# The recurrent layers of a streaming encoder on one core: 12 channel tiles of 112 against 10 of 126 and one of 84, with the gates' bias as a row

## The chip, the cores and the metric

The kernel runs on one core of a Trainium2 chip. Its engines are named PE (TensorE, matrix products), ACT (ScalarE), DVE (VectorE), POOL (GpSimd) and SP (SyncE, which here issues most of the DMA). The metric is the device time of one execution in microseconds (us); the time of a kernel is the median of several runs.

## The reference

Four layers over 256 frames of 1024 channels, batch 1. Each layer is a token mixer, a cross-attention into 256 memory tokens and a squared-ReLU MLP, each followed by `x <- LayerNorm(alpha*x + f(x))`. Layers 0 and 3 use the recurrent mixer, layer 1 a delta-rule mixer, layer 2 chunked attention. The recurrent mixer is the part that matters here; it has 1344 channels in 16 blocks of 84:

```python
u = x @ w_in                                     # 1024 -> 2 * 1344
gate_branch = gelu(u[..., :1344])
xr = causal_depthwise_conv(u[..., 1344:], conv_w, conv_b)        # 4 taps
xb = xr.reshape(bsz, seq, 16, 84)
gates = einsum('bsnc,gncd->bsgnd', xb, gate_w) + gate_b          # two gates, block-diagonal
r_gate, i_gate = sigmoid(gates)
log_a = -8 * r_gate * softplus(-lam)
a = exp(log_a)
b = sqrt(-expm1(2 * log_a)) * (i_gate * xr)
h_t = a_t * h_{t-1} + b_t                                        # scan over the frames
y = (h * gate_branch) @ w_out                    # 1344 -> 1024
```

## The kernel before

All weights come from HBM in chunks of up to 128 x 1024 float32. For each chunk ACT writes a rounded half `whi` (line 455) and DVE the rest `wlo` (line 456); a product is then three matmuls in the type fp32r, whi with both halves of the activation and wlo with the first (lines 273 to 275, `mm_piece`). `Stream` keeps up to seven split chunks: `done(i)` of a chunk lets the next be split and the raw buffer of a later one be loaded on SP's queue. Everything is issued in an order written out by hand, and each engine works through its own list in that order.

A recurrent layer (`lru`) runs over the channels in 12 tiles of 112 (`CT`), in 4 groups of 3. Three x pieces and three gelu pieces of 448 columns (`x_piece`, `g_piece`), each four chunks and two halves of 128 frames, make the two branches. `conv(i)` transposes four tiles of an x piece (line 796), ACT starts the convolution with its bias (line 802) and DVE adds three taps. `gates(g)` computes both gates of three tiles. As a block of 84 channels crosses the edges of tiles of 112, a group has seven products of 112 x 112 x 256 per gate (`GPAIRS`, line 842), in float32, into a bank of the pool `mm` (two banks); ACT adds the bias in the sigmoid and computes a tanh, per tile. The pool `acc` has four banks, `tp` two. The weights of groups 0 and 1 are loaded on SP's queue after the first x piece, those of groups 2 and 3 on ACT's queue in the middle of `gates(0)` and `gates(1)`.

`decay` and `scan` (exp, square, sqrt, DVE's scan) are issued between the halves of the gelu pieces. Last, `mem_piece` (products of the memory tokens, line 314) is drained in portions between the groups of transposes of the gelu branch (line 926); DVE multiplies (line 929), the result is split, and `out_gemm` makes the output product, 12 row tiles of 112.

In the first layer the memory tokens are loaded after the third x piece and split (`mem_split`, memhi and memlo) after `gelu(1)`; in the second recurrent layer after the first and second x piece. `lru_c`, once at the start, computes cc = -8 softplus(-lam) with a long list of small operations on POOL. `chunks` counts calls: at the sixth, the third gelu piece of the first layer, it issues the load of x itself for the residual and of the norm's two vectors.

Of the kernel before, what the change touches and what calls it, by code (L numbers as in the profile page):

```python
# [16 lines left out]
T = 256  # L17
# [3 lines left out]
CT = 112  # L21
NT = DR // CT
GPAIRS = [(0, 0), (1, 0), (0, 1), (1, 1), (2, 1), (1, 2), (2, 2)]
# [11 lines left out]
LV = 0  # L35
# [31 lines left out]
class Stream:  # L67
# [46 lines left out]
    def _split(self):  # L114
# [13 lines left out]
        for c in self._cols(i, f):  # L128
            k.split(raw[:p, c], hi[:p, c], lo[:p, c])
# [34 lines left out]
    def done(self, i):  # L164
# [68 lines left out]
class Kern:  # L233
# [20 lines left out]
    def mm_piece(self, acc, chunks, lhs, p, w, kpc=2, kt0=0, start=True, stop=True, last=False, near=None):  # L254
# [4 lines left out]
        for ci, c in enumerate(chunks):  # L259
            if not self.dry:  # L260
                wh, wl = self.st.hl[c]
                for k in range(kpc):
# [5 lines left out]
                    kt = kt0 + ci * kpc + k  # L268
                    a, b = lhs(kt)
                    ws = slice(k * w, (k + 1) * w)  # L270
# [393 lines left out]
    def out_gemm(self, name, idx, n, lhs, p):  # L664

        for nh in range(2):
            a = [self.acc(), self.acc()]
            parts = [range(n)] if n <= 4 else [range(n // 2), range(n // 2, n)]
            for part in parts:
                end = part is parts[-1]  # L670
                ch = [self.st.take(name, (*idx, nh, q), p, 1024) for q in part]
                last = end and nh == 1
                near = self.next_ht() if last else None
                for t in range(2):
                    self.mm_piece(a[t], ch, lhs[t], p, 512, kt0=2 * part[0], start=part[0] == 0, stop=end,
                                  last=t == 1 and not last, near=near if t else None)
# [98 lines left out]
    def lru(self, l, j):  # L775
        nc, tc = self.nc, self.tc
        with tc.tile_pool(name="lru", bufs=1, reuse_waits="tile") as p:
# [3 lines left out]
            nat = {}  # L781

            def x_piece(i):
                for t, a in self.gemm("lru_in", (j, 3 + i), 4, self.hT, 128, 448):
                    s = gn[t][:, 896:] if i == 2 else p.tile([128, 448], F32, name="xn", tag="CB"[i], bufs=4)
                    nc.scalar.copy(s, a[:, :448])
# [4 lines left out]
            def conv(i):  # L791
                for b in range(2):
                    ps = self.tp()
                    for q in range(2):
                        for t in range(2):
                            nc.tensor.transpose(ps[:CT, q * T + t * 128:q * T + t * 128 + 128],
                                                nat[i, t][:, (2 * b + q) * CT:(2 * b + q + 1) * CT], self.ident)
# [1145 lines left out]
```

## Time and profile before

| | us |
|---|---|
| median of 3 runs | 1813.78 (1811.99 to 1815.51) |
| the profiled execution | 1802.43 |
| its span, first to last instruction | 1800.6 |
| PE busy in it | 1736.4 (96%) |
| DVE, ACT, POOL busy | 1252.3, 871.6, 55.3 |

The stages of the first recurrent layer lie, in us from the start of the span, at 5.4 to 41.8 (x branch), to 69.2 (gates), to 100.1 (gelu branch), to 118.9 (product with the gelu branch and memory products) and to 151.6 (output product); the second recurrent layer's gates lie at 1406.5 to 1435.6 and its gelu branch at 1435.6 to 1466.1.

The mean granted clock of TensorE in that execution is 0.995 of its full 2.4 GHz. The time of one profiled execution stands below the median; it is its own run.

### The profile page before, as it was taken

How to read it: one execution, taken by the hardware profiler on the slowest of the kernel's cores; microseconds unless marked ns; L12 is line 12 of the kernel's file. 1: busy time of each engine (PE TensorE's matmuls, PEld its weight loads, DVE VectorE, ACT ScalarE, POOL GpSimd, SP SyncE). 2: the span in 40 equal slices, each digit the busy share in tenths (PEclk: the TensorE clock that was granted, in tenths of full speed). 3: DMA queues.
4: the chain of work that ended last, by engine and by line, in shares of the span. 5: the costliest groups of instructions: out<-in, count | busy, mean ns of one | idle time of the engine just before them, and what ended most of it. 6: DMA issues, size and time to landing. Idle time of an engine off the chain costs nothing.

```text
span 1800.6 us, 25667 instructions
## 1 busy us (share of the span) xinstructions
PE 1736.4 (96%) x10032; PEld 1453.8 (81%) x10032; DVE 1252.3 (70%) x1809; ACT 871.6 (48%) x1338; POOL 55.3 (3%) x64
## 2 busy tenths in 40 slices
PE   8999999999999989999999999999999999999998
PEld 7888988888777656888887888888888887988886
DVE  6587776667578798776667567776667587677665
ACT  6754534444543134544444544634444674545442
POOL 2000000000000001000000000000000000000000
PEclk9999999999999999999999999999999999999999
DMA  7464555555242224455555623545555545636552
GB/s 243 138 205 175 186 185 192 187 187 202 95 144 86 91 93 137 151 187 194 189 190 197 244 94 119 186 164 187 187 188 189 168 147 164 208 120 231 186 187 94
DMA packets 92927, 302.39 MB, mean 168 GB/s; under 512 B 11906, under 2 KB 19586, under 8 KB 92676
## 3 DMA queue, kind: packets, MB, share of 16 engines
q1 hardware_dynamic: 91780, 297.92, 49.3%
q10 hardware_dynamic: 1024, 2.81, 0.5%
q8 instruction: 79, 1.29, 0.3%
q14 instruction: 44, 0.36, 0.1%
HBM read 299.65 MB, written 1.05 MB: 167 GB/s over the span
## 4 chain that ended last, share of the span: by engine, by line
PE 78%; DVE 11%; ACT 4%; DMA 4%; issue 2%; POOL 0%; SPq 0%; DVEq 0%; ACTq 0%
PE acc L275 12%; PE acc L273 12%; PE acc L274 12%; PE tp L294 5%; PE mm L294 5%; PE acc L314 4%; PE acc L294 4%; PE acc L517 4%; PE tp L295 3%; PE mm L295 3%; DVE wlo L456 2%; PE acc L192 2%; PE mm L842 2%; PE tp L352 2%; PE acc L295 2%
## 5 line engine op out<-in xcount | busy, mean ns | idle before, releaser
L456 DVE TENSOR_TENSOR wlo<-wraw,whi 128x1024 fp32r<-128x1024 f32 (+3 forms) x505 | 593.7, 1206 | 133.3 <-ACT whi L455 121.9
L455 ACT CAST whi<-wraw 128x1024 fp32r<-128x1024 f32 (+3 forms) x505 | 507.2, 1039 | 163.5 <-PE acc L275 97.3
L273 PE MATMUL acc<-whi,ahi 128*128 128x512 f32 x512 | 200.3, 391 | 0.0
L275 PE MATMUL acc<-whi,alo 128*128 128x512 f32 x512 | 199.7, 390 | 0.0
L274 PE MATMUL acc<-wlo,ahi 128*128 128x512 f32 x512 | 199.4, 389 | 0.0
L273 PE MATMUL acc<-whi,ht 128*128 128x448 f32 (+1 forms) x368 | 142.4, 387 | 5.5 <-ACT whi L455 5.5
L274 PE MATMUL acc<-wlo,ht 128*128 128x448 f32 (+1 forms) x368 | 140.6, 382 | 3.5 <-DVE wlo L456 3.5
L275 PE MATMUL acc<-whi,ht 128*128 128x448 f32 (+1 forms) x368 | 140.4, 381 | 0.0
L294 PE MATMUL tp<-ht,whi 128*128 128x512 f32 x384 | 136.7, 398 | 0.0
L294 PE MATMUL mm<-ht,whi 128*128 128x512 f32 x384 | 136.5, 398 | 0.0
L294 PE MATMUL acc<-ht,whi 128*128 128x512 f32 x352 | 126.0, 400 | 1.9 <-DVE qkT L987 1.9
L275 PEld LDWEIGHTS acc<-whi,alo 128*128 128x128 f32 x512 | 96.1, 188 | 20.9
L273 PEld LDWEIGHTS acc<-whi,ahi 128*128 128x128 f32 x512 | 96.1, 188 | 20.2
L274 PEld LDWEIGHTS acc<-wlo,ahi 128*128 128x128 f32 x512 | 96.2, 188 | 19.2
L295 PE MATMUL tp<-ht,wlo 128*128 128x256 f32 x384 | 107.9, 281 | 0.0
L295 PE MATMUL mm<-ht,wlo 128*128 128x256 f32 x384 | 107.8, 281 | 0.0
L295 PE MATMUL acc<-ht,wlo 128*128 128x256 f32 x352 | 98.7, 280 | 0.0
L734 DVE TENSOR_TENSOR rel<-mm,rel 128x256 f32<-128x256 f32 x48 | 18.6, 425 | 110.4 <-ACT rel L733 110.4
L355 ACT CAST ht<-tp 128x512 fp32r<-128x512 f32 x40 | 22.8, 589 | 135.3 <-PE tp L352 134.3
L738 ACT CAST ahi<-rel 128x512 fp32r<-128x512 f32 x56 | 34.8, 622 | 110.0 <-DVE rel L737 110.0
L294 PEld LDWEIGHTS tp<-ht,whi 128*128 128x128 f32 x384 | 72.2, 188 | 18.0
L294 PEld LDWEIGHTS mm<-ht,whi 128*128 128x128 f32 x384 | 72.1, 188 | 17.6
(387 smaller groups left out, 3419.3 us busy)
## 6 DMA issues: line engine op xcount, KB each, us to landing
wraw<-in_w SPq DMA_DIRECT2D x256, 512.0 KB, 4.5
wraw<-in_w_kv SPq DMA_DIRECT2D x64, 512.0 KB, 4.3
wraw<-in_lru_in SPq DMA_DIRECT2D x47, 448.0 KB, 4.7
wraw<-in_w_q SPq DMA_DIRECT2D x32, 512.0 KB, 4.3
wraw<-in_w_co SPq DMA_DIRECT2D x32, 512.0 KB, 4.7
wraw<-in_ca_qkv SPq DMA_DIRECT2D x24, 512.0 KB, 4.5
wraw<-in_lru_out SPq DMA_DIRECT2D x24, 448.0 KB, 5.0
ln_gt<-in_ln_g SPq DMA_DIRECT2D x12, 512.0 KB, 6.1
```

Source lines behind the costliest of these rows:

```text
L192: return f(*a, **k)
L273: nc.tensor.matmul(acc[:, :w], lhsT=a, rhs=wh[:p, ws], start=s, stop=False)
L274: nc.tensor.matmul(acc[:, :w], lhsT=a, rhs=wl[:p, ws], start=False, stop=False)
L275: nc.tensor.matmul(acc[:, :w], lhsT=b, rhs=wh[:p, ws], start=False, stop=e)
L294: self.nc.tensor.matmul(four, lhsT=wh[:, ws], rhs=xy, start=s, stop=False)
L295: self.nc.tensor.matmul(four[:, :2], lhsT=wl[:, ws], rhs=x, start=False, stop=e)
L314: self.nc.tensor.matmul(a, lhsT=w[:, ws], rhs=v, start=s and i == 0, stop=e and i == 2)
L352: self.nc.tensor.transpose(dst_ps[:n, j * p:(j + 1) * p], s, self.ident[:p, :p])
L455: self.nc.scalar.copy(hi, src)
L456: self.nc.vector.tensor_tensor(out=lo, in0=src, in1=hi.bitcast(F32), op=ALU.subtract)
L517: nc.tensor.matmul(a, lhsT=u, rhs=w[:, ws], start=s, stop=e)
L842: nc.tensor.matmul(ps[:CT, gate * T:(gate + 1) * T], lhsT=gw[gate][:, n, :], rhs=xc[g][:, k, :], start=n == ks[0][0], stop=n == ks[-1][0])
```

## The change

The channels of the recurrent layers are reordered when the weights are laid out. Three blocks of 84 make two tiles of 126: each tile has one whole block and one half (42 channels) of the third, the first tile's half at rows 0 to 41, the second tile's at rows 64 to 105. Five such pairs and the last block alone, 84, make 11 tiles, in groups of 4, 4 and 3. A tile's gates are then one full product, and for each pair and gate two products of 42 rows bring what the divided block owes to the other tile. The tiles of xc have one row more, which holds 1.0; the gate weights hold the bias in that row. All pieces are 504 or 336 columns, and `mm_piece` steps over a pitch of 64 so that the split halves of 504 columns lie at a pitch of 512. The output product ends in a chunk of one short tile. Order: gates(0), conv(2), tanh(0), (first layer: mem_split), gates(1), tanh(1), gates(2), tanh(2). Sigmoid runs on both gates of a tile at once, cc is multiplied in by DVE, tanh and exp run on a whole group.

```diff
-CT = 112
-NT = DR // CT
-GPAIRS = [(0, 0), (1, 0), (0, 1), (1, 1), (2, 1), (1, 2), (2, 2)]
+CT = 126
+NT = 11
+LB = 84
+LW = 504, 504, 336
...
+        w = f // 2
+        if _pitch(w) == w or f <= 512:
+            for c in self._cols(i, f):
+                k.split(raw[:p, c], hi[:p, c], lo[:p, c])
+        else:
+            for q in ((0, 1), (1, 2)) if i == 0 else ((0, 2),):
+                at = lambda x, n: x[:p, :2 * n].rearrange("p (k w) -> p k w", w=n)[:, q[0]:q[1], :w]
+                k.split(at(raw, w), at(hi, _pitch(w)), at(lo, _pitch(w)))
...
+def _pitch(w):
+    return -(-w // 64) * 64
...
+                if tail and ci == n - 1:
+                    p, kpc, ci0 = tail, 1, 2 * ci
+                else:
+                    ci0 = ci * kpc
...
-                    ws = slice(k * w, (k + 1) * w)
+                    ws = slice(k * _pitch(w), k * _pitch(w) + w)
...
+            tiles = 4, 4, 3
+            wide = lambda c: LB if c == NT - 1 else CT
...
-            xc = [p.tile([CT, 3, T], F32, name="xc", tag="A", bufs=4) for _ in range(4)]
+            xc = [p.tile([CT + 1, n, T], F32, name="xc", tag=f"A{g}") for g, n in enumerate(tiles)]
+            for x in xc:
+                nc.gpsimd.memset(x, 1.0)
...
             def load_gw(g, queue):
-                gws.append([])
-                for gate in range(2):
-                    w = p.tile([CT, 7, CT], F32, name="gw", tag="gw", bufs=4)
-                    queue.dma_start(w, self.I["lru_gw"][j, g, gate])
-                    gws[g].append(w)
+                m = tiles[g] + tiles[g] // 2
+                w = p.tile([CT + 1, 2, m * CT], F32, name="gw", tag=f"gw{g}")
+                queue.dma_start(w, self.I["lru_gw"][j, g, :, :, :m * CT])
+                gws.append(w)
 
             def gates(g):
-                for o in range(3):
-                    ps = self.acc() if LV & 8 else self.mm()
-                    ks = [(n, k) for n, (k, oo) in enumerate(GPAIRS) if oo == o]
+                n, gw = tiles[g], gws[g]
+                r = p.tile([CT, 2, n, T], F32, name="ri", tag=f"B{g}")
+                for b in range(2):
+                    os = range(2 * b, min(2 * b + 2, n))
+                    bank = (self.mm, self.acc)[b]
+                    pss = [bank() for _ in os]
                     for gate in range(2):
-                        for n, k in ks:
-                            nc.tensor.matmul(ps[:CT, gate * T:(gate + 1) * T], lhsT=gw[gate][:, n, :], rhs=xc[g][:, k, :],
-                                             start=n == ks[0][0], stop=n == ks[-1][0])
-                    c = 3 * g + o
-                    nc.scalar.activation(r[:, o, :], ps[:CT, :T], AF.Sigmoid, bias=par[:, c, 6:7])
-                    nc.scalar.activation(it[:, o, :], ps[:CT, T:], AF.Sigmoid, bias=par[:, c, 7:8])
-                    nc.scalar.activation(h[:, o, :], r[:, o, :], AF.Tanh, scale=cc[:, c:c + 1])
-                nc.vector.tensor_tensor(out=xc[g], in0=xc[g], in1=it, op=ALU.mult)
-                if g < 2:
-                    load_gw(g + 2, nc.scalar)
+                        gs = slice(gate * T, (gate + 1) * T)
+                        for o, ps in zip(os, pss):
+                            nc.tensor.matmul(ps[:CT, gs], lhsT=gw[:, gate, o * CT:(o + 1) * CT], rhs=xc[g][:, o, :],
+                                             start=True, stop=len(os) == 1)
+                        if len(os) == 1:
+                            continue
+                        w = slice((n + b) * CT, (n + b + 1) * CT)
+                        for u in range(2):
+                            a = slice(64 * u, 64 * u + 42)
+                            nc.tensor.matmul(pss[1 - u][:CT, gs], lhsT=gw[a, gate, w], rhs=xc[g][a, 2 * b + u, :], start=False, stop=True)
+                    for o, ps in zip(os, pss):
+                        nc.scalar.activation(r[:, :, o, :], ps[:CT, :].rearrange("p (g t) -> p g t", g=2), AF.Sigmoid)
+                v = r[:, 0, :n, :]
+                nc.vector.tensor_tensor(out=v, in0=v, in1=cc[:, 4 * g:4 * g + n].unsqueeze(2).to_broadcast([CT, n, T]), op=ALU.mult)
+                x = xc[g][:CT, :n, :]
+                nc.vector.tensor_tensor(out=x, in0=x, in1=r[:, 1, :n, :], op=ALU.mult)
+                ri.append(r)
+
+            def tanh(g):
+                nc.scalar.activation(ri[g][:, 1], ri[g][:, 0], AF.Tanh)
...
             x_piece(0)
-            for g in range(2):
+            for g in range(3):
                 load_gw(g, nc.sync)
...
-            else:
-                conv(2)
-                gates(1)
...
+            gates(0)
+            conv(2)
+            tanh(0)
+            if l == 0:
+                self.mem_split()
+            gates(1)
+            tanh(1)
             gates(2)
-            gates(3)
...
-            else:
-                g0 = g_piece(0, lambda t: (decay(2 * t), decay(2 * t + 1)))
+            tanh(2)
+            g0 = g_piece(0, lambda t: (decay(0), decay(1)) if t == 0 else decay(2))
...
-            else:
-                g1 = g_piece(1, lambda t: (scan(2 * t), scan(2 * t + 1)))
+            g1 = g_piece(1, lambda t: (scan(0), scan(1)) if t == 0 else scan(2))
             gelu(0, gn)
             gelu(1, g1)
-            if l == 0:
-                self.mem_split()
             gelu(2, g_piece(2))
...
-            self.out_gemm("lru_out", (j,), 6, [lhs(0), lhs(1)], CT)
+            self.out_gemm("lru_out", (j,), 6, [lhs(0), lhs(1)], CT, tail=("lru_out2", LB))
```

## Rows read from the trace of the kernel before

**Rows 1.** Page, part 1: busy us of each engine, share, instructions.

```profile
PE 1736.4 (96%) x10032; PEld 1453.8 (81%) x10032; DVE 1252.3 (70%) x1809; ACT 871.6 (48%) x1338; POOL 55.3 (3%) x64
```

**Rows 2.** Windows: PE, PEld, DVE, ACT, POOL busy, granted clock, DMA share, GB/s.

```profile
5.40:41.80 36.40, 34.91 (x160) 30.04 (x161) 26.25 (x43) 22.84 (x36) 10.64 (x24) 1.00 0.82 269
41.80:69.20 27.40, 25.38 (x121) 20.35 (x120) 12.34 (x21) 17.86 (x40) 0.00 (x0) 1.00 0.53 157
69.20:100.10 30.90, 29.80 (x146) 27.10 (x145) 23.68 (x29) 29.08 (x42) 0.00 (x0) 1.00 0.39 135
100.10:118.90 18.80, 16.00 (x121) 15.60 (x120) 15.01 (x19) 7.73 (x11) 0.00 (x0) 0.91 0.74 222
118.90:151.60 32.70, 32.23 (x144) 26.39 (x142) 23.93 (x29) 13.81 (x16) 1.00 (x1) 1.00 0.64 200
1406.50:1435.60 29.10, 27.14 (x123) 22.02 (x122) 14.60 (x27) 20.41 (x43) 0.00 (x0) 0.94 0.42 138
1435.60:1466.10 30.50, 29.41 (x145) 26.80 (x144) 23.62 (x29) 27.40 (x40) 0.00 (x0) 1.00 0.39 129
```

**Rows 3.** Timeline of PE in the first layer's gates: start, us, instruction, count.

```profile
47.92 1.04 PE L796 MATMUL tp<-ident,gn 128*112 128x128 f32 x8
48.80 6.21 PE L842 MATMUL mm<-xc,gw 112*112 112x256 f32 x28
```

**Rows 4.** Timeline of PE, products of 64 rows: attention twice, then the delta rule.

```profile
1044.73 0.28 PE L314 MATMUL acc<-memhi,wlo 128*128 128x256 f32 x1
1044.85 0.28 PE L314 MATMUL acc<-memhi,whi 128*128 128x256 f32 x1
1045.06 1.13 PE L1014 MATMUL mm<-qkT,qkT 64*128 64x256 f32 x4
1046.12 0.39 PE L314 MATMUL acc<-memlo,whi 128*128 128x256 f32 x1
...
1026.91 1.16 PE L1014 MATMUL mm<-qkT,qkT 64*128 64x128 f32 x8
...
564.39 2.06 PE L192 MATMUL acc<-ar,ht 64*128 64x128 f32 x32
```

**Rows 5.** Groups by line and shape: attention's products of 64 rows (busy us, mean ns).

```profile
L1014 PE MATMUL mm<-qkT,qkT 64*128 64x256 f32 x32 | 9.0, 402 | 0.0
```

**Rows 6.** Waits of PE, first layer and then second: total us, times, longest.

```profile
PE acc L314 <- DVE memlo L456: 2.8, 1, 2.8
PE mm L842 <- DMA gw<-in_lru_gw: 2.0, 2, 1.6
PE acc L274 <- DVE wlo L456: 1.5, 3, 1.1
...
PE mm L842 <- ACT it L846: 2.0, 1, 2.0
PE tp L926 <- DVE xc L929: 1.6, 1, 1.6
PE acc L274 <- DVE wlo L456: 1.1, 1, 1.1
```

**Rows 7.** First convolution: ACT's timeline, POOL's last lru_c row, POOL's 256-element memset.

```profile
25.39 1.94 ACT L802 ACTIVATE xc<-tp,par 112x256 f32<-112x256 f32 x4 [0.20 <-PE tp L796]
...
28.19 0.27 POOL L971 TENSOR_SCALAR cc<-cc 112x24 f32<-112x24 f32 x1
...
L1223 POOL MEMSET tw<- 1x256 f32 x1 | 0.3, 305 | 0.1
```

**Rows 8.** First layer, timelines of DVE, SP's queue and ACT around the output weights.

```profile
91.66 4.34 DVE L456 TENSOR_TENSOR wlo<-wraw,whi 128x896 fp32r<-128x896 f32 x4
94.13 0.90 SPq L250 DMA_DIRECT2D h<-in_x  x2
105.29 1.05 ACT L455 CAST whi<-wraw 112x1024 fp32r<-112x1024 f32 x1 [6.38 <-DMA wraw<-in_lru_out]
108.94 1.01 DVE L929 TENSOR_TENSOR xc<-xc,tp 112x512 f32<-112x512 f32 x2
```

More of the change, by code (lines that the diff above doesn't have):

```diff
@@ L252, in chunks, with mm_piece @@
         return [self.st.take(name, (*idx, q), p, f) for q in range(n)]
-    def mm_piece(self, acc, chunks, lhs, p, w, kpc=2, kt0=0, start=True, stop=True, last=False, near=None):
+    def mm_piece(self, acc, chunks, lhs, p, w, kpc=2, kt0=0, start=True, stop=True, last=False, near=None, tail=None):
         nc = self.nc
@@ L670, in out_gemm @@
                 end = part is parts[-1]
-                ch = [self.st.take(name, (*idx, nh, q), p, 1024) for q in part]
+                short = tail is not None and end
+                ch = [self.st.take(name, (*idx, nh, q), p, 1024) for q in part[:len(part) - short]]
+                if short:
+                    ch.append(self.st.take(tail[0], (*idx, nh), tail[1], 512))
                 last = end and nh == 1
@@ L675, in out_gemm @@
                     self.mm_piece(a[t], ch, lhs[t], p, 512, kt0=2 * part[0], start=part[0] == 0, stop=end,
-                                  last=t == 1 and not last, near=near if t else None)
+                                  last=t == 1 and not last, near=near if t else None, tail=tail[1] if short else None)
                     if last and t == 0:
@@ new lines, in tanh @@
+            def tanh(g):
+                nc.scalar.activation(ri[g][:, 1], ri[g][:, 0], AF.Tanh)
+            def decay(g):
+                n = tiles[g]
+                a, h = ri[g][:, 0], ri[g][:, 1]
+                a2 = p.tile([CT, 4, T], F32, name="a2", tag="C")[:, :n, :]
+                nc.scalar.activation(a, a, AF.Exp)
+                nc.scalar.activation(a2, a, AF.Square)
+                nc.vector.scalar_tensor_tensor(out=h, in0=a2, scalar=1.0, in1=h, op0=ALU.add, op1=ALU.mult)
+            def scan(g):
+                n = tiles[g]
+                h, x = ri[g][:, 1], xc[g][:CT, :, :]
+                nc.scalar.activation(h, h, AF.Sqrt, scale=-1.0)
+                nc.vector.tensor_tensor(out=h, in0=h, in1=x, op=ALU.mult)
+                for o in range(n):
+                    nc.vector.tensor_tensor_scan(xc[g][:CT, o, :], ri[g][:, 0, o, :], ri[g][:, 1, o, :], 0.0, ALU.mult, ALU.add)
@@ L1913, in prep @@
         gw[:, :, sl, sl] = g["lru_gate_w"][:, :, n]
-    gt = np.zeros((2, 4, 2, CT, 7, CT), np.float32)
-    for q in range(4):
-        for n, (k, c) in enumerate(GPAIRS):
-            k0, c0 = (3 * q + k) * CT, (3 * q + c) * CT
-            gt[:, q, :, :, n, :] = gw[:, :, k0:k0 + CT, c0:c0 + CT]
+    gw, gb = gw[:, :, order][:, :, :, order], gb[:, :, order]
+    gt = np.zeros((2, 3, CT + 1, 2, 6 * CT), np.float32)
+    for c in range(NT):
+        k = slice(c * CT, min((c + 1) * CT, DR))
+        n, at = k.stop - k.start, (c % 4) * CT
+        gt[:, c // 4, :n, :, at:at + n] = gw[:, :, k, k].transpose(0, 2, 1, 3)
+        gt[:, c // 4, CT, :, at:at + n] = gb[:, :, k]
+    for q in range(5):
+        x, y = 2 * q * CT, (2 * q + 1) * CT
+        at = ((4, 3)[q == 4] + q % 2) * CT
+        gt[:, q // 2, 0:42, :, at:at + CT] = gw[:, :, x:x + 42, y:y + CT].transpose(0, 2, 1, 3)
+        gt[:, q // 2, 64:106, :, at:at + CT] = gw[:, :, y + 64:y + 106, x:x + CT].transpose(0, 2, 1, 3)
     o["lru_gw"] = gt
```

136 lines of the change are left out of this document (57 added, 79 removed).

## Prediction

> **What bounds the kernel now.** I read the page first: TensorE (PE) is busy 96% of the span [rows 1], so what PE executes or waits for in the two recurrent layers is the time to look at. The table of stages comes next [rows 2]: the x branch, the gates, the gelu branch and the product with the gelu branch. Three things are to be seen in it. In the gates PE is the long engine, while ScalarE (ACT) and VectorE (DVE) have slack (17.9 and 12.3 of 27.4 us). In the gelu branch ACT works 29.1 of 30.9 us, so it can become the bound there. The granted clock is 0.91 in one stage and 0.94 in another; between the two levels, 2.4 and 1.2 GHz, that is 18% of 18.8 us and 12% of 29.1 us at the lower level, about 3.4 us each, and half of it, 1.7 us each, is lost. Both follow a wait of PE, which the view of waits names [rows 6]. Last I read PE in order of time and by shape, for the price of one instruction [rows 3 to 5].
>
> **Gates, removed.** A float32 product of 256 columns stands in the trace as two passes: 14 products of a group are 28 instructions, which take 6.21 us, so one pass costs (6.21 - 0.38) / 27 = 0.216 us [rows 3]. 56 products per layer are 112 passes: 24.2 us.
>
> **Gates, added.** 22 full products, 44 passes at 0.216: 9.5 us (127 rows instead of 112 change no row of a pass). Then ten sets per layer (five pairs of tiles, two gates) of two products with 42 rows, at rows 0 and 64, into two banks. The trace has no 42-row product; the nearest have 64 rows. Four passes on the same half of the rows take 1.13 us, a pitch of 0.25; the first starts 0.21 after a product whose own pitch is 0.12, and the next stage starts 1.06 after it, so entering costs 0.09 and leaving 0.05 [rows 4]. Whether the two halves run beside each other, two rows of equal shape tell: with one half only, 8 passes of 128 columns take 1.16 us, 0.127 each; with the halves in turn 32 take 2.06 us, 0.058 each. So they overlap. A set is A1 A2 B1 B2, in that order; only A2 and B1 can meet. That is three pitches: 0.09 + 3 x 0.25 + 0.05 = 0.89 us. Without overlap it is 1.14, with complete overlap 0.64. I take 0.89: ten are 8.9 us, the gates 18.4 us, a saving of 5.8 us per layer (3.3 to 8.3).
>
> These rows show that a change of the row mode costs 0.14 us in and out [rows 4]. The Trainium skill (TensorEngine Tiling (Array Packing), Key Properties) says that a change of the tiling mode drains the engine, which speaks against this change: with a full drain of about 0.16 us (a pass lasts 0.40 but is followed after 0.25) at both ends, an estimate from rows 4 and 5, a set would be near 1.07 us and the forecast 3.6 us higher. The trace agrees that there is a price, and puts it lower.
>
> **Fewer tiles.** The output product has 11 instead of 12 row tiles: 12 of 144 matmuls go, at 32.7 / 144 = 0.227 each [rows 2], 2.7 us per layer. Four transposes of 48 go, at (1.04 - 0.27) / 7 = 0.11 [rows 3]: 0.4 us. The input product keeps its 288 matmuls and all columns; 448 columns cost 29.8 / 146 = 0.204, 512 cost 0.227 [rows 2], 256 cost 0.12 [rows 4], nearly a straight line, so 192 of 504 and 96 of 336 give 0 to -0.6 us; I take -0.3.
>
> **Waits that go** [rows 6]. First layer: the second half of the gate weights was loaded from ACT's queue in the middle of the gates and PE waited 2.0 us; all three loads are now issued after the first x piece, 20 us ahead. mem_split moves from the gelu branch to behind tanh(0), where DVE has room, so the wait for memlo, 2.8 us, goes, with 1.7 us of clock. Second layer: PE waited 2.0 us for the sigmoids to free one of two banks; half the tiles now use the other pool of four. That and its 1.7 us of clock go. In each layer a wait of 1.1 us for a late weight split goes, since DVE leaves the gates earlier. ACT has 11 sigmoids, 3 tanh where there were 36 instructions; the bias rides in the extra row of the full products. DVE gains three multiplies by cc, about 1.0 us each (two of 512 elements take 1.01 [rows 8]), covered by its slack in the gates [rows 2]; without it they cost 3 us per layer. The temporary of `decay` has one buffer instead of two: ACT's second square waits about 1 us for DVE, behind PE's first gelu piece. The moved loads stand on SP's queue (2.1 MB instead of 1.4, 2.4 us at 269 GB/s [rows 2]) ahead of the gelu branch's chunks, which are needed 25 us later, and in the second layer ahead of the memory tokens, whose split holds ACT 2.4 us longer; what of that reaches PE is in (d).
>
> **Waits that come.** (a) The memsets of xc queue on GpSimd (POOL) behind the constants of lru_c, which end at 28.46 us [rows 7]. Four times the 256-element row, 1.2 us, makes xc[0] ready at 29.7. The first convolution on ACT, at 25.39 now and about 27 with the larger first piece, waits 2.7 us; behind it on ACT stand the splits of the last x chunks. I take 1.2 us of it for PE (0 to 2.7). (b) The first four chunks are 57 KB larger each, 0.85 us at 269 GB/s [rows 2]; with what PE does meanwhile, +0.5. (c) Behind tanh(0) ACT now waits for the memory tokens before the next sigmoids: +0.3. (d) In the second layer gates(1) still needs a bank that ACT frees after its splits and table load: +0.8. (e) The costly one. In the first layer the load of x goes out at 94.13 us, after DVE's split of the last input chunk (the second of the four from 91.66). The output weights queue behind it, their cast ends ACT's wait at 105.29, and DVE does its first product at 108.94 behind their split [rows 8]; PE's second group of transposes needs that. I estimate this chain 8.0 us earlier (7 for the gates' end, 1 for the shorter lists) while PE comes 11.9 us earlier: a wait of 3.9 us and again 1.7 us of clock.
>
> **Sum.** First layer: gates -5.8, transposes -0.4, output -2.7, input -0.3, waits -2.0, -1.1, -2.8 and -1.7 = -16.8; new +1.2, +0.5, +0.3 = -14.8; (e) +5.6: -9.2 us. Second layer: -5.8, -0.4, -2.7, -0.3, -2.0, -1.7, -1.1, and 0.7 of the 1.6 us wait for xc = -14.7; (d) +0.8: -13.9 us. Together -23.1 us. The profiled execution took 1802.4 us (1800.6 of span) and would take 1779.3. The runs' median is 1813.8, 11.4 above it; I carry the difference over: 1790.7 us.
>
> **Rivals.** (1) The halves overlap completely (0.64 per set, -5.0 us) or chain (e) arrives with PE (-5.6): 1780 to 1786 us. For it speaks the 0.058 us row, against it the order of the four passes. The Trainium skill (TensorE: Matmul & The Clock Gate, Part 3: Packing small matmuls) has products of different row groups run concurrently; by that rule the forecast would be 1785.7. Chance 0.18. (2) The halves do not overlap (+5.0), or a chain like (e) also holds the second layer (+5.6), whose ACT is busy 27.4 of 30.5 us: 1796 to 1803. Chance 0.20. (3) The change of mode makes every short pass wait for the one before, its whole 0.40 us [rows 5] and once more to leave: 2.0 us per set, gates 29.5 us per layer, +22 us on the forecast, 1812.9: no change. The four passes in 1.13 us speak against it. Chance 0.06. (4) Slower: the clock. If PE's sparser 42-row passes dropped the granted clock to 1.2 GHz for the gates of both layers, 2 x 18.4 us would be doubled: +36.8, 1827 us; it turns the sign once more than 23 of these 36.8 us are at the lower level. Against it: the gates now run at 1.00 and 0.94, the latter after a wait [rows 2]. The Trainium skill (TensorE: Matmul & The Clock Gate, Part 1: The HAM clock gate) names an activity monitor as what sets this clock. Chance 0.05.
>
> **How the numbers follow.** The forecast has 0.51, on its own 1786 to 1796. The range 1780 to 1803 takes in rivals 1 and 2, so the bounds of the half products and of the waits, and leaves out 3 and 4, with what lies beyond the bounds. About 0.2%, 3.6 us, is what a measurement can tell from no change. Faster: the forecast and rivals 1 and 2, 0.89; within 0.2%: 0.06; slower: 0.05.
>
> **What the next profile would show.** 44 + 40 gate passes per layer instead of 112, the half sets at 0.9 us; stages of the gates near 19.5 us; no wait for gw or memlo; a first convolution held by POOL's memset until about 29.7 us; a PE wait of about 4 us in the first layer's product with the gelu branch; 132 output matmuls per layer. Wrong would make it: half sets above 1.2 us, a granted clock below 0.9 in the gates, or waits for DVE or ACT of more than 5 us in the gelu branch.

## The result, and the profile after

The changed kernel takes 1957.74 us (median of 4 runs, 1956.84 to 1958.47) against 1812.88 us for the kernel before (4 runs, 1809.22 to 1815.51): a ratio of 1.079, 95% interval 1.076 to 1.082. The forecast was 1790.7 us. It is 7.9% slower where 1.3% faster was expected.

The page of the kernel after, part 1 (as [rows 1]) and the first lines of part 4, the chain of work that ended last:

```profile
PE 1755.4 (90%) x9944; PEld 1441.9 (74%) x9944; DVE 1249.7 (64%) x1795; ACT 850.3 (43%) x1268; POOL 60.1 (3%) x70
...
PE 71%; DVE 11%; SPq 8%; ACT 4%; DMA 3%; issue 2%; POOL 0%; DVEq 0%; ACTq 0%
```

PE is busy 90% of the span, not 96%: it waits. The last chain names a resource that the prediction priced at 2.4 us and that has 0% in the chain of the kernel before: SP's queue, 8% of 1956.2 us, some 156 us. The view of PE's waits (as [rows 6]) says where:

```profile
PE tp L829 <- ACT xn L818: 72.1, 1, 72.1
PE tp L829 <- ACT whi L472: 46.3, 1, 46.3
PE mm L874 <- DMA gw<-in_lru_gw: 15.4, 1, 15.4
```

Three waits, one in the first layer and two in the second, hold 133.8 us. The first two name ACT, but ACT is itself idle; its own longest waits are for weight chunks and for the memory tokens (waits of ACT):

```profile
ACT memhi L472 <- DMA kT<-in_memT: 84.3, 4, 75.4
ACT whi L472 <- DMA wraw<-in_lru_in: 83.1, 11, 74.9
```

The DMA queue of SP in the first layer (start, us, instruction, count; the last line is the first of the eight chunks above it by itself), and the windows of the same time (as [rows 2]):

```profile
12.10 10.25 SPq L107 DMA_DIRECT2D wraw<-in_lru_in  x6
22.40 42.30 SPq L860 DMA_DIRECT2D gw<-in_lru_gw  x3
64.81 55.07 SPq L107 DMA_DIRECT2D wraw<-in_lru_in  x8
...
64.81 30.52 SPq L107 DMA_DIRECT2D wraw<-in_lru_in  x1
```

```profile
40.00:60.00 20.00, 0.00 (x0) 0.00 (x0) 0.00 (x0) 0.00 (x0) 0.00 (x0) 0.51 0.06 27
60.00:80.00 20.00, 0.00 (x0) 0.00 (x0) 0.00 (x0) 0.00 (x0) 0.00 (x0) 0.50 0.06 26
```

This is the reading that matters. While every engine stands still, the DMA share is 0.06, which is one sixteenth, and 26 to 27 GB/s move: one of the 16 DMA engines works. It works on the three loads of the gates' weights (750, 750 and 500 KB, 2.05 MB together; at 26.5 GB/s 77 us). Their issue holds SP's queue for 0.28, 13.1 and 28.8 us, one after the other, and that of the first chunk behind them for 30.5 us, from 64.81 to 95.3; ACT's wait of 74.9 us for this chunk ends at 107.59. The [rows 2] stream, whose chunks have 128 partitions, moves 269 GB/s; the gates' weights now have 127. The Trainium skill (DMA: Bandwidth & Descriptors, Why a DMA increments its semaphore by 16 and not by 1) says that a transfer is spread over the largest number of engines, at most 16, that divides the slowest dimension of both its sides, and gives 127 partitions as its example for one engine. The trace agrees: 0.06 of the engines, 26 GB/s.

What the prediction looked at is there, near the forecast in its total though not in its parts. PE in the first layer's gates, in order of time (as [rows 3]):

```profile
117.18 1.03 PE L874 MATMUL mm<-xc,gw 127*126 127x256 f32 x4
118.14 0.70 PE L881 MATMUL mm<-xc,gw 42*126 42x256 f32 x4
118.77 1.13 PE L874 MATMUL mm<-xc,gw 127*126 127x256 f32 x4
119.83 0.70 PE L881 MATMUL mm<-xc,gw 42*126 42x256 f32 x4
120.46 1.13 PE L874 MATMUL acc<-xc,gw 127*126 127x256 f32 x4
```

Four full passes and a set of half-row passes recur after 1.69 us (118.77 to 120.46). Less 4 x 0.216, a set costs 0.83 us; forecast 0.89.

Narrow windows of the timeline show when single passes start, in the kernel after and then in the kernel before, where attention's four passes of [rows 4] all use one half:

```profile
117.83 0.38 PE L874 MATMUL mm<-xc,gw 127*126 127x256 f32 x1
118.14 0.48 PE L881 MATMUL mm<-xc,gw 42*126 42x256 f32 x2
118.46 0.38 PE L881 MATMUL mm<-xc,gw 42*126 42x256 f32 x2
```

```profile
1045.06 0.48 PE L1014 MATMUL mm<-qkT,qkT 64*128 64x256 f32 x1
1045.38 0.38 PE L1014 MATMUL mm<-qkT,qkT 64*128 64x256 f32 x1
1045.59 0.38 PE L1014 MATMUL mm<-qkT,qkT 64*128 64x256 f32 x1
```

The four half-row passes start as two pairs, 0.01 us apart within a pair: the halves run fully beside each other, in two steps and not in three. The change between full and half rows (the row mode) is dearer than forecast: from the last full pass to the first pair are 0.31 us, from pair to pair 0.32, to the next full pass 0.31 (118.77) and from there to its successor 0.32, each 0.10 above the 0.216 of a pass. That is 0.40 us per set, where the prediction took 0.14; 2 x 0.216 + 0.40 is the 0.83 measured. The kernel before already shows it: of its four passes the second starts 0.32 after the first and the third 0.21 after the second, which the prediction averaged into a pitch of 0.25.

### The profile page after: what moved, and what is told of

It reads as the page before. It is cut to its first block, busy times and chain, and to the rows that moved or that the text cites. A ratio compares the mean times of both kernels' runs of the same rounds, so it can differ in the third digit from the quotient of the medians.

```text
span 1956.2 us, 25405 instructions
## 1 busy us (share of the span) xinstructions
PE 1755.4 (90%) x9944; PEld 1441.9 (74%) x9944; DVE 1249.7 (64%) x1795; ACT 850.3 (43%) x1268; POOL 60.1 (3%) x70
## 4 chain that ended last, share of the span: by engine, by line
PE 71%; DVE 11%; SPq 8%; ACT 4%; DMA 3%; issue 2%; POOL 0%; DVEq 0%; ACTq 0%
PE acc L292 11%; PE acc L290 11%; PE acc L291 11%; PE mm L311 4%; PE tp L311 4%; SPq L860 4%; PE acc L534 3%; PE acc L311 3%; PE acc L331 3%; PE tp L312 2%; PE mm L312 2%; DVE wlo L473 2%; PE acc L204 2%; PE tp L369 2%; SPq L460 2%
## 5 line engine op out<-in xcount | busy, mean ns | idle before, releaser
L473 DVE TENSOR_TENSOR wlo<-wraw,whi 128x1024 fp32r<-128x1024 f32 (+5 forms) x505 | 592.5, 1203 | 225.3 <-ACT whi L472 222.7
L472 ACT CAST whi<-wraw 128x1024 fp32r<-128x1024 f32 (+5 forms) x505 | 506.2, 1036 | 253.1 <-PE acc L292 103.8
L290 PE MATMUL acc<-whi,ht 128*128 128x512 f32 (+2 forms) x368 | 146.0, 397 | 5.4 <-ACT whi L472 5.4
L291 PE MATMUL acc<-wlo,ht 128*128 128x512 f32 (+2 forms) x368 | 143.7, 391 | 4.9 <-DVE wlo L473 4.9
L292 PE MATMUL acc<-whi,ht 128*128 128x512 f32 (+2 forms) x368 | 143.2, 389 | 0.0
L290 PEld LDWEIGHTS acc<-whi,ht 128*128 128x128 f32 x368 | 71.6, 194 | 20.4 <-ACT whi L472 6.1
L291 PEld LDWEIGHTS acc<-wlo,ht 128*128 128x128 f32 x368 | 71.3, 194 | 20.5 <-DVE wlo L473 6.8
```

The lines of the kernel that those rows point to most:

```text
L290: nc.tensor.matmul(acc[:, :w], lhsT=a, rhs=wh[:p, ws], start=s, stop=False)
L291: nc.tensor.matmul(acc[:, :w], lhsT=a, rhs=wl[:p, ws], start=False, stop=False)
L292: nc.tensor.matmul(acc[:, :w], lhsT=b, rhs=wh[:p, ws], start=False, stop=e)
L472: self.nc.scalar.copy(hi, src)
L473: self.nc.vector.tensor_tensor(out=lo, in0=src, in1=hi.bitcast(F32), op=ALU.subtract)
```

## Experiments

Theory T: the 127 partitions put each load on one engine; that is the loss, and the rest behaves as forecast. Rivals: R1, the place of the loads on SP's queue; R2, their bytes and long rows; R3, the half-row products and the new order.

**128 rows.**

```diff
-                w = p.tile([CT + 1, 2, m * CT], F32, name="gw", tag=f"gw{g}")
+                w = p.tile([CT + 2, 2, m * CT], F32, name="gw", tag=f"gw{g}")
...
-    gt = np.zeros((2, 3, CT + 1, 2, 6 * CT), np.float32)
+    gt = np.zeros((2, 3, CT + 2, 2, 6 * CT), np.float32)
```

(and the full products read `gw[:CT + 1]`.) 

> The changed kernel, with one more row, of zeros, in the gates' weight array and tile, so that its three loads per layer have 128 partitions instead of 127; the products read the first 127 rows as before, and every load stands where it stood. Theory T (a load of 127 partitions is carried by one of the 16 DMA engines, here at 26.5 GB/s; PE waits for it and for the weight chunks behind it, some 167 us over both layers): the loads move at the rate of the others, all three of 2.07 MB within 10 us, no wait of PE above 6 us in the recurrent layers, and the rest of the prediction holds: about 1790 us, 1780 to 1803. Rival R1 (the place of the loads is at fault: 2 MB on SP's queue ahead of the chunks) and rival R2 (their bytes and their rows of 3 KB from far-apart places): nothing of this changes, so 1950 to 1958 us. Rival R3 (the half-row products and the new order in the gates cost the time): also 1950 to 1958.

Measured: 1805.92 us (1801.61 to 1809.30), ratio 0.9957 (0.9943 to 0.9972). One row of zeros more takes 151.8 us off. R1 and R3 fall as the main cause, since the place and the products are unchanged, and so does R2. SP's queue in that run:

```profile
22.93 1.59 SPq L860 DMA_DIRECT2D gw<-in_lru_gw  x3
24.63 22.94 SPq L107 DMA_DIRECT2D wraw<-in_lru_in  x8
```

The issue of the three loads takes 1.59 us, not 42.30. But T is not the whole: the time is 15 us above the 1790 expected.

**The same bytes in two loads.**

```diff
-                queue.dma_start(w, self.I["lru_gw"][j, g, :, :, :m * CT])
+                for rows in (slice(0, CT), slice(CT, CT + 1)):
+                    queue.dma_start(w[rows], self.I["lru_gw"][j, g, rows, :, :m * CT])
```

> The changed kernel, with each load of the gates' weights issued as two: 126 rows, and the one bias row by itself. Bytes, rows, place and products are the same. Theory T: only the count of partitions matters. 126 is divisible by 14, so 14 engines carry it, at about 14 x 26.5 = 371 GB/s at most; the single row of 3 to 6 KB is one engine's 0.2 us and a fixed delay. About 1790 us, within 5 us of the version with 128 rows. R1, R2, R3: 1950 to 1958 us, as nothing that they name has changed.

Measured: 1818.41 us, ratio 1.0024 (1.0011 to 1.0036). It removes 139 us, as T says, but stays 12.5 us behind the 128 rows, not 5. In the second layer the memory tokens come later (ACT waits 4.8 us for them instead of 1.1), so PE waits twice around its gates, and the windows behind show the price, the granted clock being the third number from the right:

```profile
1426.23 0.77 PE L829 MATMUL tp<-ident,gn 128*126 128x128 f32 x5 [1.08 <-ACT gn L818]
1428.18 1.87 PE L875 MATMUL mm<-xc,gw 127*126 127x256 f32 x4 [1.19 <-issue]
```

```profile
1420.00:1440.00 20.00, 17.72 (x60) 9.75 (x61) 14.86 (x27) 11.70 (x17) 0.00 (x0) 0.71 0.43 157
1440.00:1460.00 20.00, 20.00 (x66) 13.98 (x63) 7.11 (x7) 11.81 (x14) 0.00 (x0) 0.69 0.00 1
```

At 0.71 and 0.69 PE loses 0.29 and 0.31 of 20 us, 12 us in all, behind 2.3 us of waiting. Part of that comes back, because the version with 128 rows waits longer later on: from the first input product to the end of the output product its layers take 144.5 and 136.9 us, those of the two-load version 148.4 (PE waits 2.1 us more in the x branch) and 144.7, so 11.6 of the 12.5 us are 3.9 in the first layer and 7.7 in the second. R1 has a small truth: the loads ahead of the memory tokens leave little room.

How two short waits came to cost that much, the granted clock shows, in the two-load version and then in the kernel before, behind its wait of 2.0 us:

```profile
1446.00:1448.00 2.00, 2.00 (x7) 1.17 (x8) 0.00 (x0) 0.98 (x2) 0.00 (x0) 0.50 0.00 0
1452.00:1454.00 2.00, 2.00 (x9) 1.62 (x9) 0.00 (x0) 1.98 (x3) 0.00 (x0) 0.94 0.00 0
```

```profile
1416.00:1418.00 2.00, 2.00 (x9) 1.67 (x8) 1.26 (x2) 1.88 (x5) 0.00 (x0) 0.51 1.04 391
1418.00:1420.00 2.00, 2.00 (x11) 1.65 (x10) 2.00 (x6) 1.30 (x4) 0.00 (x0) 1.00 0.91 268
```

In the two-load version PE worked through the gates from 1430 to their end at 1448.4 at 1.2 GHz, and the clock rose only in the gelu branch. The kernel after shows the same in its second layer: 0.50 to the end of the gates at 1589.7, and 1.00 at 1594 to 1598. In the kernel before the clock was back within the gates. Whether it is the half-row sets that keep it down is not shown; no run takes them apart from the rest of the stage.

**The kernel before, with 127 partitions.**

```diff
-                    w = p.tile([CT, 7, CT], F32, name="gw", tag="gw", bufs=4)
+                    w = p.tile([127, 7, CT], F32, name="gw", tag="gw", bufs=4)
...
-    gt = np.zeros((2, 4, 2, CT, 7, CT), np.float32)
+    gt = np.zeros((2, 4, 2, 127, 7, CT), np.float32)
```

(and the products read `gw[gate][:CT]`.) 

> The kernel before, with only its loads of the gates' weights enlarged from 112 to 127 partitions (15 more rows of zeros in the array; the products read the first 112 rows, every instruction else is as before). Each of the eight loads per layer grows from 351 to 398 KB. Theory T: each takes 398 KB / 26.5 GB/s = 15 us on one engine; the four ahead of the gates 60 us together on that engine and the chunks behind them wait for it, and the four on ACT's queue come later by up to 60 us too: 60 to 120 us per layer less some 20 us of lead, so 1890 to 2010 us. R1, R2 and R3 (place, row pitch, half-row products): none of them is in this kernel, and 13% more bytes are under 1 us of the whole queue: 1812 to 1818 us.

Measured: 2033.06 us (one run), 220 us above its before, 23 us more than the upper end that T gave. PE waits 106.7 us for gw itself, and while the first four loads run the windows show the same sixteenth:

```profile
50.00:70.00 20.00, 0.00 (x0) 0.00 (x0) 0.00 (x0) 0.00 (x0) 0.00 (x0) 0.50 0.06 26
```

T holds with nothing else of the change in the kernel.

**The missing 15 us.** The waits of PE in the run with 128 rows are no longer than forecast by more than a few us, but equal instructions have other mean times, in every layer. Groups by line and shape, dense layers, the kernel before (busy us, mean ns):

```profile
L273 PE MATMUL acc<-whi,ahi 128*128 128x512 f32 x512 | 200.3, 391 | 0.0
L294 PE MATMUL mm<-ht,whi 128*128 128x512 f32 x384 | 136.5, 398 | 0.0
```

and in the kernel after:

```profile
L290 PE MATMUL acc<-whi,ahi 128*128 128x512 f32 x512 | 202.8, 396 | 0.0
L311 PE MATMUL mm<-ht,whi 128*128 128x512 f32 x384 | 134.6, 391 | 0.0
```

The first kind (split weights moving, activations stationary) lost 5 ns a pass, the second (activations moving) gained 7. The dense layers' code is untouched; what differs is the place of their tiles. The constants par and cc shrank from 768 + 96 to 528 + 88 bytes per partition, 864 to 640 as placed (in steps of 32), and everything allocated behind them, the activations of all layers, stands 224 bytes lower. The weight chunks, allocated from the other end, stayed. Theory L: the place sets the pace.

```diff
+            self.c_p.tile([128, 56], F32, name="gap")
             self.hT = _LazyT(self)
```

(224 bytes; `[128, 8]`, 32 bytes, in the kernel before.) The version with 128 rows, shifted back: 

> The version with 128 rows, with an unused tile of 224 bytes per partition among the constants, so that every tile placed behind them has the address that it has in the kernel before. (The constants par and cc became smaller with the change: 864 bytes of placed tiles became 640. So all tiles behind them, the activations of every layer among them, stand 224 bytes lower, and their addresses went from odd to even multiples of 32 bytes, while the weight chunks, placed from the other end, kept odd ones.) Nothing else differs. Theory L (the place of the tiles sets the pace of TensorE's passes): the 512-column passes with split weights as moving and activations as stationary operand, 396 ns each in the version with 128 rows and 390 in the kernel before, go back to 390; those with activations as moving operand, 391, go back to 398. By the groups that both kernels have: +8.3 for the second product of the dense layers, +2.7, +2.3, -4.3, +1.9 is 10.9 us, and about 4 us more in the recurrent layers' own products: 15 us, so 1791 us (1787 to 1795). Rival: the 5 to 6 ns come from the chip or the day, and the missing 15 us from waits in the recurrent layers: 1803 to 1809 us, mean times unchanged.

The kernel before, shifted by 32 bytes: 

> The kernel before, with an unused tile of 32 bytes per partition among the constants, so that every tile behind them stands 32 bytes higher, at an even multiple of 32 bytes. Every instruction is as before. Theory L: the passes with split weights moving and activations stationary go from 390 to 396 ns, the others from 398 to 391, so by the same groups 10.9 us and some 4 us more: 1824 to 1829 us. Rival (no effect of the place): 1810 to 1816 us and the mean times of before.

The version with 128 rows, its weights shifted by 32 bytes instead (an unused tile ahead of the chunks): 

> The version with 128 rows, with an unused tile of 32 bytes ahead of the weight chunks at the other end of the memory, so that chunks, split weights and memory tokens also stand at even multiples of 32 bytes: all operands now have the same phase, and all are even. Theory L in a first form (moving and stationary operand should have the same phase, odd or even): 390 ns for the passes with split weights moving, as in the kernel before, and about 1791 us. In a second form (each operand has its own cost, and the split weights as moving operand stay at 396 whatever they meet): 1806 us. In a third form (a moving operand at an odd multiple costs 7 ns, which the passes with moving activations showed by 398 against 391): both kinds fast, 389 to 391, and 1787 us or less. Rival (no effect of the place): 1803 to 1809 us.

Measured: 1792.90 us (ratio 0.9891, 0.9874 to 0.9908), 1823.94 us (1.0067, 1.0051 to 1.0084), and 1808.29 us (0.9973, 0.9962 to 0.9983). Both directions hold: shifting back gains 13.0 us, and 32 unused bytes in the kernel before, with not one instruction changed, cost 11.0 (by the medians; by the two ratios both are 12). The groups follow; first the version shifted back, then the kernel before with 32 bytes:

```profile
L290 PE MATMUL acc<-whi,ahi 128*128 128x512 f32 x512 | 200.3, 391 | 0.0
L311 PE MATMUL mm<-ht,whi 128*128 128x512 f32 x384 | 136.5, 398 | 0.0
```

```profile
L273 PE MATMUL acc<-whi,ahi 128*128 128x512 f32 x512 | 202.8, 396 | 0.0
L294 PE MATMUL mm<-ht,whi 128*128 128x512 f32 x384 | 134.6, 391 | 0.0
```

To the last tenth these are the kernel before's and the kernel after's own values. The passes overlap, so their recorded lengths are not their pace, but from start to start the same holds: the kernel before against the kernel before with 32 bytes, the first kind goes from 229 to 234 ns, the second from 236 to 230. Which form of L is right was open, so the fourth combination of odd and even multiples of 32 bytes, and two more odd ones:

> The fourth combination of places: the version with 128 rows, activations at odd multiples of 32 bytes (224 bytes of unused tile among the constants) and weight chunks, split weights and memory tokens at even ones (32 bytes of unused tile at the other end). Known so far, for passes of 512 columns with split weights moving: 390 ns (activations, stationary, odd; weights odd), 396 (even; odd), 396 (even; even). Theory S (the stationary operand's place sets it): 390 ns for these; and for the passes with activations moving and split weights stationary, known as 398 (activations odd, weights odd), 391 (even, odd), 395 (even, even): a value at or above 398. So within 4 us of the version shifted back, 1789 to 1797 us, plus up to 3 for the second kind. Rival (the two must both be odd): 396 ns, and 1803 to 1810 us.

> The kernel before, with an unused tile of 64 bytes per partition among the constants: every tile behind them stands 64 bytes higher, again at an odd multiple of 32 bytes, but at another distance from the weight chunks. If odd multiples on both sides are what makes the passes with split weights moving fast (odd with odd 390 ns, the three other combinations 396): 389 to 391 ns for the second product of the dense layers, 398 for the passes with activations moving, and the time of before, 1808 to 1818 us. If it is the distance between the two operands (65 x 1024 bytes in the kernel before, no whole multiple of 64 in the two slow cases with unlike phases): 395 to 396 ns, and about 1824 us.

> The version with 128 rows, with an unused tile of 96 bytes per partition among the constants instead of 224: the activations stand 128 bytes lower than in the kernel before, at odd multiples of 32 bytes, and at a third distance from the weight chunks. Odd with odd: 389 to 391 ns and 1789 to 1796 us. Distance: 395 to 396 ns and 1803 to 1809 us.

Measured: 1803.85 us (0.9959, 0.9945 to 0.9973) with 396 ns; 1827.38 us (one run) with 396 ns; 1808.51 us (one run) with 395 ns. Theory S falls, and so does the reading by odd and even: two odd-with-odd placements are slow. What orders all kernels so far is the distance between the split weights and the activations, modulo 256 bytes (counted as 0 in the kernel before): where that residue is equal, the mean times are equal, whichever side was moved. Residues 192 and 224 were reached in two and three ways; 0 is one placement in two kernels, and 128 rests on one run. The four residues not yet seen, on the version with x later (below):

> The version with x later, with 64 bytes of unused tile among the constants instead of 224, so that the activations stand 160 bytes lower than in the kernel before: a distance between weight chunks and activations of 160, modulo 256, larger. So far the means of the passes followed that distance modulo 256 alone (weights moving / activations moving: 0 gives 390/398, 128 gives 395/393, 192 gives 396/395, 224 gives 396/390, and equal residues gave equal means whichever side was moved). If residue 0 alone is fast for the first kind: 395 to 396 and 391 to 396, and 1783.4 + 11 to 15: 1794 to 1799 us.

> The same with 128 bytes, a residue of 96. If residue 0 alone is fast for the passes with weights moving: 395 to 396 ns, and 1794 to 1799 us.

> The same with 160 bytes, a residue of 64. If residue 0 alone is fast for the passes with weights moving: 395 to 396 ns, and 1794 to 1799 us. If the neighbourhood of the residue 0 counts: between 390 and 396.

> The same with 192 bytes, a residue of 32. If residue 0 alone is fast for the passes with weights moving: 395 to 396 ns, and 1794 to 1799 us. If the neighbourhood of the residue 0 counts, this is the nearest to it: 390 to 393 ns and under 1790 us.

Measured: 1798.58 us (0.9914, 0.9892 to 0.9936), 1795.54 (0.9894, 0.9878 to 0.9911), 1791.73 (0.9867, 0.9852 to 0.9881), 1795.75 (0.9892, 0.9877 to 0.9906), where residue 0 gives 0.9837. Mean ns of the groups:

| residue | whi,ahi | whi,alo | wlo,ahi | ht,whi | kernels |
|---|---|---|---|---|---|
| 0 | 391 | 390 | 389 | 398 | before, shifted back, x later |
| 32 | 396 | 395 | 395 | 393 | x later, 192 bytes |
| 64 | 389 | 394 | 392 | 397 | x later, 160 bytes |
| 96 | 399 | 394 | 392 | 392 | x later, 128 bytes |
| 128 | 395 | 395 | 394 | 393 | 128 rows, 96 bytes |
| 160 | 397 | 396 | 396 | 394 | x later, 64 bytes |
| 192 | 396 | 395 | 395 | 395 | weights by 32; before by 64 |
| 224 | 396 | 396 | 395 | 391 | after; 128 rows; before by 32; both moved |

Residue 0 is the best of the eight for the first kind over its three columns (390 on average, 392 at residue 64, which has the lowest single value), and the worst for the second; the first kind is the larger part of this kernel by busy time. The kernel before stood on it. The neighbours 32 and 224 are as slow as the rest; 64 lies between, and so does its time.

**The load of x one piece later,** on the version shifted back: step (e) of the prediction.

```diff
-            self.gb_due = 6
+            self.gb_due = 7
```

> As the version with 128 rows and the tiles shifted back, and the load of x and of the first layer norm's rows issued one piece later in the first layer, behind the first output-weight chunks on SP's queue instead of ahead of them. By the prediction's step (e) (the output weights queue behind the load of x, which ends in a wait of PE of 5.4 us in the first layer's product with the gelu branch, and a lower clock behind it): that wait shrinks to under 2 us, 4 to 6 us less than the version shifted back: 1786 us (1782 to 1789). Rival: the wait comes from DVE's own chain of scans and splits and not from the load; then the time is within 2 us of the version shifted back.

Measured: 1783.41 us (1780.69 to 1784.79), ratio 0.9837 (0.9820 to 0.9853): 9.5 us less, where 4 to 6 were expected. PE's wait in the first layer's product with the gelu branch, shifted back and then with x later:

```profile
106.53 1.97 PE L947 MATMUL tp<-ident,gn 128*126 128x128 f32 x8 [8.17 <-DVE xc L950]
```

```profile
99.98 1.26 PE L947 MATMUL tp<-ident,gn 128*126 128x128 f32 x8 [0.96 <-DVE xc L950]
```

The chain of the output weights was right, its length not: PE, faster with the shift undone, met it 8.2 us early. No version is clear of this one, 1.6% below the kernel before.

**Two smaller waits,** each on the version with x later: POOL's fills of xc ahead of lru_c, and the scans of groups 1 and 2 half a piece later.

```diff
             for x in xc:
                 nc.gpsimd.memset(x, 1.0)
+            if j == 0:
+                self.lru_c()
```

```diff
-            g1 = g_piece(1, lambda t: (scan(0), scan(1)) if t == 0 else scan(2))
+            g1 = g_piece(1, lambda t: (root(0), root(1), scan(0)) if t == 0 else (root(2), scan(1)))
...
-            gelu(2, g_piece(2))
+            gelu(2, g_piece(2, lambda t: scan(2) if t == 0 else None))
```

(`lru_c` no longer runs at the start of the kernel; `root(g)` is the square root with which `scan(g)` began, issued by itself.)

> As the version with x later, and POOL's fills of xc issued ahead of the constants of lru_c, not behind them. By the prediction's step (a) the first convolution waits for the fill (2.4 to 2.5 us of ACT) and PE gets 1.2 us of it (0 to 2.7). Without that wait: 1 to 1.5 us less than the version with x later, 1782 us. Rival (PE's 1.0 us for a late weight split there has another cause): no difference, 1783.4.

> As the version with x later, and the scans of groups 1 and 2 each issued half a piece of the gelu branch later (the square roots on ACT stay where they are), so that DVE splits the weights of the third gelu piece before the second group's scan and not after it. In the version with x later PE waits for that split 2.04 us in the first layer and 1.86 in the second, where the granted clock of the next 20 us is 0.91, so 0.9 us more. The prediction said that this wait (1.1 us in each layer) would go. Theory D (DVE's order makes it: its scans are as long as before and the gates ahead of them are shorter): 4 to 5 us less, 1779 us. Rival (DVE is full there, the split's wait moves to the scans' readers in the product with the gelu branch): 1782 to 1785.

Both together: 

> As the version with x later, with both: the fills of xc first and the scans apart. If the two gains add up: 1 to 1.5 and 4 to 5 us, 1777 to 1779 us. Rival (one of them only moves a wait): 1780 to 1783.

Measured: 1783.74 us (0.9848, 0.9826 to 0.9869), 1786.37 (0.9852, 0.9834 to 0.9870) and 1783.38 (0.9843, 0.9826 to 0.9859). None differs from x later. The fills: PE's wait of 0.98 us in the x branch goes and the first layer ends 1.0 us earlier in the trace, too little for these runs to show. The scans: the wait for wlo, 2.04 us in the x-later version, goes, and another takes its place; the row of x later first, then the one of the scans apart:

```profile
88.31 0.42 PE L291 MATMUL acc<-wlo,ht 128*128 128x336 f32 x1 [2.04 <-DVE wlo L473]
```

```profile
99.69 1.97 PE L949 MATMUL tp<-ident,gn 128*126 128x128 f32 x8 [2.51 <-DVE xc L952]
```

DVE is full through the gelu branch, and what is moved off one reader meets the next; theory D falls and the rival's mechanism holds, though the time lies 1.4 us above the rival's range.

Not tried: the half products of both gates in one go, which would halve the changes of the row mode (at 0.40 us for each of ten sets, an estimate of 2 us per layer); it would open a second accumulation in a bank while one is unfinished.

## Why the prediction was wrong, point by point

**The step that failed** is the one on the moved loads: "The moved loads stand on SP's queue (2.1 MB instead of 1.4, 2.4 us at 269 GB/s [rows 2])". The bytes and the place were right; the rate was that of another shape. A load of 127 partitions moves 26 GB/s, and the term is +151.8 us (kernel after against 128 rows), 133.8 of it the three waits. Most of the rest is the clock behind them: in the second layer PE works 12.65 us at 0.51 and 20.00 us at 0.50 (busy time and granted clock), half of which, 16 us, is lost:

```profile
1490.00:1530.00 40.00, 12.65 (x32) 6.68 (x32) 0.00 (x0) 0.00 (x0) 0.00 (x0) 0.51 0.06 26
...
1570.00:1590.00 20.00, 20.00 (x53) 10.91 (x51) 8.41 (x14) 7.41 (x13) 0.00 (x0) 0.50 0.16 57
```

(windows of the kernel after, as [rows 2]). The diff showed the `CT + 1`, and the prediction read it only as "127 rows instead of 112 change no row of a pass". No rival had a transfer as its mechanism.

**A step that was missing:** the working prices only what the recurrent layers do, and takes every other pass at its old time. Shrinking par and cc moved the tiles of all layers, and their passes cost 13.0 us more (128 rows against shifted back). No row of the trace before could have given the size; that the constants became smaller was in the diff.

**The rest.** With both taken out the time is 1792.9 us, against 1813.0 of its before: -20.1 us where the sum said -23.1, and inside the range. The three parts, -20.1, +13.0 and +151.8, make +144.7, the 144.9 measured. That the rest came so near is in part luck. The sum was worked out on the trace, and on the traces the two recurrent layers, each from its first input product to the end of its output product, take 148.1 and 143.9 us before and 144.7 and 132.7 in the version shifted back: -3.4 where -9.2 was forecast, and -11.2 where -13.9 was, together 8.5 short. The profiled execution of the kernel before lies 11.4 us below its median, that of the version shifted back 2.2 below; where the other executions of the kernel before lose the difference, no trace shows.

- *Half-row sets:* 0.83 us each against 0.89 taken, right by luck. The prediction took three steps of 0.25 and 0.14 for the change of row mode; the traces have two steps of 0.216 and 0.40, and the two errors nearly cancel. Rival 1 had the complete overlap right and, with 0.64, the same price of the change too low. That the trace puts this price below 0.16 us at each end does not hold: it is 0.20. Rival 2 on the halves and rival 3 (2.0 us a set) did not come. In the version with 128 rows the first layer's gates last 18.6 us (42.96 to 61.59), with 19.5 forecast and 27.4 before [rows 2].
- *Clock in the gates* (rival 4): full in the version with 128 rows (the window is the first layer's). But where a wait let it fall, as in the two-load version's second layer, it stayed at 1.2 GHz to the end of the gates, which is part of what rival 4 feared:

```profile
40.00:60.00 20.00, 19.64 (x103) 12.76 (x101) 18.32 (x30) 15.20 (x23) 0.00 (x0) 1.00 0.64 204
```

- *Fewer tiles:* 88 of each of the three output passes for two layers, 132 per layer, as counted; the output product is 2.1 us shorter in each layer, with 2.7 taken.
- *Waits that go:* those for gw, for memlo and for the sigmoids' bank are gone. Those for wlo are not: 2.6 and 1.9 us in the version shifted back instead of 1.1 and 1.1 [rows 6]. The step took DVE to be early because it leaves the gates early; its scans then stand ahead of the split just the same. By its own count that is 2 x 1.1 not saved and 2.3 added.
- *(a), fills of xc:* ACT waits 2.4 to 2.5 us as forecast (2.7); of PE's 1.2 us, 1.0 is seen in the trace and none in the runs.
- *(e), the output weights:* mechanism right, 3.9 us taken, 8.2 measured, and 9.5 us with the clock behind it.
- *(d), the second layer:* the loads ahead of the memory tokens cost little with 128 rows, but the two-load version shows how near that was: tokens 3.8 us later came with 7.7 us more in that layer.

The two terms that came out too dear, (e) with 4.3 us and wlo with 4.5, are together about the 8.5 us that the traced layers fell short; by this count the others nearly cancel.

## What to carry to other kernels

Read the partition count of every load that a change touches before its bytes: with 127 rows 2 MB took 77 us, and one row more took these away. A pitch read from a merged row of the timeline is an average: read single passes where a price at the edges is to be told from one in the middle. When a change resizes anything that is allocated early, compare the mean time of untouched instructions in both traces first, since a shift of all later tiles shows there and nowhere in the waits. A wait that is costed at its own length is costed too low where PE's clock falls behind it.

## What the runs showed of the hardware

- One DMA engine moves 26 to 27 GB/s here. The issue of three loads that ran on one held SP's queue for 42.3 us, and that of the next chunk for 30.5, so that loads with 128 partitions behind them were late as well.
- Products on different halves of the rows ran fully beside each other (starts 0.01 us apart), and changing between full and half rows cost 0.20 us each way.
- The pace of a 512-column pass depends on the distance in memory between moving and stationary tile: 389 to 399 ns for one kind, 391 to 398 for the other, by the distance modulo 256 bytes, with equal times at equal residues (192 and 224 were reached in two and three ways, the others have one placement each). What in the memory makes it so stays open; the passes with memory tokens, which stand at the same end as the weights, kept 392 to 397 ns in all versions but three (397 to 402: x later and two of its shifts, where a few of these passes ran at 1.2 GHz).
- Waits of 1.1 and 1.2 us close together were followed by some 24 us at 1.2 GHz in the two-load version, to the end of the gates and into the gelu branch, and a single wait of 2.0 us by none that the windows of x later show in the first layer (1.00 at 80 to 100 us), though the 1.9 us in the second gave 0.91 (1440 to 1460 us). What makes the difference stays open.
